# Gate and up of a SwiGLU by Strassen's product, in a one-core transformer layer

## The chip, the core and the metric
The kernel runs on one core of a Trainium2 chip: TensorE (PE, with its weight loads shown as PEld), VectorE (DVE), ScalarE (ACT), GpSimd (POOL) and SyncE (SP), which here issues the DMAs. The metric is the time of one execution on the device in microseconds (us). The core has an on-chip memory of 128 partitions (SBUF) and eight banks of 2 KB a partition (PSUM) into which PE accumulates.

## The reference
One decoder layer on 512 tokens and 16 meta tokens, 1024 channels: sparse attention, a residual and LayerNorm, a SwiGLU of width 2816, a residual and LayerNorm.

```python
def swiglu(h, w_gate, w_up, w_down):
    return (jax.nn.silu(h @ w_gate) * (h @ w_up)) @ w_down
...
h = layer_norm(DEEPNORM_ALPHA * h + mix, ln1_g[i], ln1_b[i])
ffn = swiglu(h, ffn_w_gate[i], ffn_w_up[i], ffn_w_down[i])
h = layer_norm(DEEPNORM_ALPHA * h + ffn, ln2_g[i], ln2_b[i])
```

All is float32. h is (512, 1024), w_gate and w_up are (1024, 2816), w_down is (2816, 1024).

## The kernel before
Each product is made of three matmuls of fp32r parts: a float32 operand x is split into hi, a copy of x on ACT (`act_copy`, L156), and lo = x - hi, a subtraction on DVE or POOL (`sub`, L159); the product is hi*hi + hi*lo + lo*hi (`mm3`, L286 to L288).

The order of the work is the order of the program: `manual_schedule` keeps each engine's instructions as the code issues them, and every engine works its own list from front to back, waiting on semaphores where an operand or a buffer isn't ready. Tiles come from pools by tag with a fixed count of buffers: `q` has 8 (four rows of 528 each), `u` 28, `kq` 14, `lg` 2, the weights `wraw`, `whi` and `wlo` 3 each, and PSUM has the tags `mm` 2, `S` 3, `pt` 2, `av` 1.

After attention come three stages. In the first, the output projection of the second half of the channels goes token block by token block (L968 to L978, blocks b of 128 tokens); `residual` and `norm` work on DVE, POOL and ACT, and `turn_norm` transposes a normalised block on PE and splits it into h1h and h1l. In the second (L991 to L1015), for each of 22 blocks f of 128 columns of w_gate and w_up, PE makes gate into p_wg and up into p_wu, 24 matmuls of 512 tokens each (block 0 in two halves of 256 tokens, so that it can begin before blocks 2 and 3 are normalised). `ahead` loads chunks of weights (128 x 1024) two ahead and cuts one ahead: ACT copies h_wg and h_wu, DVE makes l_wg, POOL l_wu. ACT takes silu of p_wg (L1004), DVE multiplies by p_wu (L1005), and the product is split into hh and hl. At the last block `ahead("wd0_0")` has the first chunk of w_down cut (L1002). In the third (L1037 to L1083), PE multiplies hh and hl with w_down into pd, in two halves th of 256 tokens, and DVE, POOL and ACT do the last normalisation.

Of the kernel before, what the change touches and what calls it, by code (L numbers as in the profile page):

```python
# [117 lines left out]
def trunk(ctx, tc, a, out):  # L118
# [839 lines left out]
    def turn_norm(b):  # L958
        for q in range(2):
            pt = bank(f"tz{b}{q}", "pt")  # L960
            for i in range(4):
# [4 lines left out]
            sub(nc.vector, lo, ptv, hi)

    for b in range(NB):  # L968
        if b:
            po[1, b] = bank(f"po1{b}", "mm")  # L970
        for k in range(0 if b else 6, KT):
            out_terms(1, k, b)
            if b > 1 and k == LATE:
                turn_norm(b - 2)
        residual(1, b)
        norm(b)
        if b == 0:
            load(g_ff, 2)  # L978


    hh, hl = [], []
    hq = []

    def widen(nm, o, n0, n1):
        wh, wl = chunk(nm)
        return mm3(
            o[:, n0:n1],
            ((wh[:, k * P : (k + 1) * P], wl[:, k * P : (k + 1) * P], h1h[k][:, n0:n1], h1l[k][:, n0:n1]) for k in range(KT)),
        )

    for f in range(NF):  # L991
        pg = [bank(f"p_wg{f}", "mm"), bank(f"p_wu{f}", "S")]

        for n0, n1 in ((0, 2 * P), (2 * P, S)) if f == 0 else ((0, S),):
            for o, nm in zip(pg, (f"wg{f}", f"wu{f}")):
                if n1 == S:
                    ahead(nm)
                for k, _ in enumerate(widen(nm, o, n0, n1)):
                    if n1 < S and k == LATER_K:
                        turn_norm(2 + (nm == "wu0"))  # L1000
        if f == NF - 1:
            ahead("wd0_0")  # L1002
        sg = third(f"sg{f}")[:, :S]
        nc.scalar.activation(sg, pg[0], AF.Silu)  # L1004
        nc.vector.tensor_tensor(out=sg, in0=pg[1], in1=sg, op=ALU.mult)  # L1005
        if f < 8:
            if f % 4 == 0:
                hq.append((quad(f"hh{f}", S), quad(f"hl{f}", S)))
            hi, lo = (x[:, f % 4] for x in hq[f // 4])
        else:  # L1010
            hi, lo = unit(f"hh{f}", F32R)[:, :S], unit(f"hl{f}", F32R)[:, :S]
        act_copy(hi, sg)
        sub(nc.vector, lo, sg, hi)
        hh.append(hi)
        hl.append(lo)  # L1015
# [129 lines left out]
```

## Time and profile before

| | us |
|---|---|
| median of 3 executions | 688.37 (687.09 to 688.86) |
| the profiled execution | 688.74 |
| its span | 687.0 |
| PE, DVE, ACT, POOL busy in the span | 668.5, 418.3, 287.6, 244.8 |
| output projection's end to the first down product | 312.4 to 556.4 |
| down products | 556.4 to 672.7 |

Times in rows count from the span's start. The span runs from the first to the last instruction; the execution's own time has some 1.7 us more around it. A busy engine is one that works on an instruction, and a matmul's row is longer than the distance to the next, since matmuls are pipelined: the pace is read from start to start.

### The profile page before, as it was taken

Reading aid. Unit: us, or ns where it says so; the run is one execution under the profiler, and the core shown is the slowest. Engines: PE = TensorE matmul, PEld = TensorE weight load, DVE = VectorE, ACT = ScalarE, POOL = GpSimd, SP = SyncE. Lnnn points to the kernel's source line nnn. Section 1 sums busy time; section 2 is a strip of 40 time slices with the busy share of each in tenths; the row PEclk is TensorE's granted clock in tenths of the full one; section 3 lists DMA queues with packets and bytes.
Section 4 is the critical chain, followed back from the end, with each engine's and each line's share of the span. In section 5 each row is a group of like instructions: output and inputs, shape, how many; then the busy total and the mean of one; then the engine's idle time right before and its main releaser. Section 6 shows DMA issues by size and latency. Waiting matters only on the chain.

```text
span 687.0 us, 9443 instructions
## 1 busy us (share of the span) xinstructions
PE 668.5 (97%) x3440; PEld 564.2 (82%) x3440; DVE 418.3 (61%) x788; ACT 287.6 (42%) x516; POOL 244.8 (36%) x249
## 2 busy tenths in 40 slices
PE   7999999999999999999999999999999999999995
PEld 5888787888998888888888888888888888888884
DVE  5589897898888887686334233343433355575425
ACT  5573512567767675513323233232322344423310
POOL 2063802597786776654212122221212200011004
PEclk9999999999999999999999999999999999999998
DMA  6557131542223245410131322313132267745601
GB/s 235 172 167 253 42 75 37 153 139 79 71 85 109 71 135 189 154 61 29 65 122 62 124 80 104 119 66 123 63 121 90 94 231 234 238 148 198 208 32 61
DMA packets 31806, 83.11 MB, mean 121 GB/s; under 512 B 3744, under 2 KB 8912, under 8 KB 31760
## 3 DMA queue, kind: packets, MB, share of 16 engines
q1 hardware_dynamic: 31328, 82.12, 36.6%
q8 instruction: 27, 0.44, 0.3%
q10 hardware_dynamic: 432, 0.39, 0.2%
q14 instruction: 19, 0.16, 0.1%
HBM read 74.86 MB, written 5.27 MB: 117 GB/s over the span
## 4 chain that ended last, share of the span: by engine, by line
PE 85%; DVE 6%; POOL 3%; ACT 2%; issue 2%; DMA 1%; SPq 0%; POOLq 0%; DVEq 0%; ACTq 0%
PE pd L1063 17%; PE p_wu L287 6%; PE p_wu L286 6%; PE p_wu L288 6%; PE p_wg L287 6%; PE p_wg L286 6%; PE p_wg L288 6%; PE po L771 3%; PE av L726 3%; PE pv L288 2%; PE pv L286 2%; PE pv L287 2%; PE pt L696 2%; PE p_q L288 2%; PE p_q L287 2%
## 5 line engine op out<-in xcount | busy, mean ns | idle before, releaser
L159 POOL TENSOR_TENSOR l_wu<-r_wu,h_wu 128x1024 fp32r<-128x1024 f32 x22 | 52.9, 2405 | 179.5 <-ACT h_wu L156 179.5
L1005 DVE TENSOR_TENSOR sg<-p_wu,sg 128x512 f32<-128x512 f32 x22 | 15.2, 692 | 107.6 <-PE p_wu L288 107.6
L159 DVE TENSOR_TENSOR l_wd<-r_wd,h_wd 128x1024 fp32r<-128x1024 f32 x36 | 45.4, 1263 | 41.2 <-ACT h_wd L156 41.1
L287 PE MATMUL p_wg<-h1l,h_wg 128*128 128x512 f32 (+1 forms) x184 | 70.0, 380 | 0.3 <-DVE h1l L159 0.3
L286 PE MATMUL p_wg<-h1h,h_wg 128*128 128x512 f32 (+1 forms) x184 | 70.0, 381 | 0.0
L286 PE MATMUL p_wu<-h1h,h_wu 128*128 128x512 f32 (+1 forms) x184 | 70.0, 380 | 0.0
L288 PE MATMUL p_wu<-h1h,l_wu 128*128 128x512 f32 (+1 forms) x184 | 69.9, 380 | 0.0
L287 PE MATMUL p_wu<-h1l,h_wu 128*128 128x512 f32 (+1 forms) x184 | 69.9, 380 | 0.0
L288 PE MATMUL p_wg<-h1h,l_wg 128*128 128x512 f32 (+1 forms) x184 | 69.9, 380 | 0.0
L159 DVE TENSOR_TENSOR l_wg<-r_wg,h_wg 128x1024 fp32r<-128x1024 f32 x21 | 52.9, 2518 | 24.4 <-ACT h_wg L156 24.4
L156 ACT ACTIVATE hh<-sg 128x512 fp32r<-128x512 f32 x22 | 13.9, 633 | 119.7 <-DVE sg L1005 119.7
L670 POOL TENSOR_TENSOR lg<-lg,rec 128x144 f32<-128x144 f32 (+1 forms) x64 | 52.6, 846 | 21.9 <-DVE rec L668 21.1
L1063 PE MATMUL pd<-h_wd,hh 128*128 128x512 f32 (+1 forms) x162 | 59.6, 368 | 0.0
L1063 PE MATMUL pd<-h_wd,hl 128*128 128x512 f32 (+1 forms) x162 | 59.6, 368 | 0.0
L1063 PE MATMUL pd<-l_wd,hh 128*128 128x512 f32 (+1 forms) x162 | 59.5, 368 | 0.0
L156 ACT ACTIVATE h_wd<-r_wd 128x1024 fp32r<-128x1024 f32 x36 | 38.1, 1061 | 45.6 <-DMA r_wd<-in_wd 23.2
L644 POOL TENSOR_TENSOR bm<-score,tz 128x256 f32<-128x256 f32 (+1 forms) x64 | 43.9, 717 | 16.4 <-DVE mn L653 14.9
L938 POOL TENSOR_TENSOR fr<-fr,half_neg 128x1 f32<-128x1 f32 x4 | 4.0, 992 | 116.0 <-DVE fr L937 116.0
L661 ACT ACTIVATE lg<-lg,mn 128x272 f32<-128x272 f32 (+1 forms) x64 | 36.3, 571 | 11.6 <-DVE mn L653 11.6
L287 PEld LDWEIGHTS p_wg<-h1l,h_wg 128*128 128x128 f32 x184 | 34.6, 188 | 7.0 <-DVE h1l L159 0.5
L286 PEld LDWEIGHTS p_wg<-h1h,h_wg 128*128 128x128 f32 x184 | 34.6, 188 | 6.9 <-ACT h1h L156 0.2
L288 PEld LDWEIGHTS p_wu<-h1h,l_wu 128*128 128x128 f32 x184 | 34.6, 188 | 6.6
(333 smaller groups left out, 1759.4 us busy)
## 6 DMA issues: line engine op xcount, KB each, us to landing
r_wd<-in_wd SPq DMA_DIRECT2D x36, 512.0 KB, 4.2
r_wg<-in_wg SPq DMA_DIRECT2D x22, 512.0 KB, 3.7
r_wu<-in_wu SPq DMA_DIRECT2D x22, 512.0 KB, 4.5
kb<-ka SPq DMA_DIRECT2D x32, 132.0 KB, 2.3
r_wq<-in_wq SPq DMA_DIRECT2D x8, 512.0 KB, 4.8
r_wk<-in_wk SPq DMA_DIRECT2D x8, 512.0 KB, 3.4
rbig<-rdram SPq DMA_DIRECT2D x1, 3072.0 KB, 15.2
hTr<-in_hT SPq DMA_DIRECT2D x8, 264.0 KB, 5.2
```

The lines of the kernel that those rows point to most:

```text
L156: nc.scalar.activation(o, i, AF.Copy, scale=scale)
L159: eng.tensor_tensor(out=o, in0=x, in1=y.bitcast(F32), op=ALU.subtract)
L286: nc.tensor.matmul(o, lh, rh, start=i == 0, stop=False)
L287: nc.tensor.matmul(o, lh, rl, start=False, stop=False)
L288: nc.tensor.matmul(o, ll, rh, start=False, stop=i == KT - 1)
L644: nc.gpsimd.tensor_tensor(out=bm.at(b, W[b] - n, W[b]), in0=mask.at(b, W[b] - n, W[b]), in1=tzs[h][:, 256 - n :], op=ALU.add)
L661: nc.scalar.activation(lg.blk(b), lg.blk(b), AF.Exp, bias=mn[:, i : i + 1], scale=-1.0, accum_out=den[:, b : b + 1])
L670: nc.gpsimd.tensor_tensor(out=lg.blk(b), in0=lg.blk(b), in1=rec[:, b : b + 1].to_broadcast([P, W[b]]), op=ALU.mult)
L726: nc.tensor.matmul(av[:, 512 - w :], lhs, x[:, c : c + w], start=u == 0 and z == 0, stop=u == 4 and z == len(pr) - 1,)
L771: nc.tensor.matmul(po[hf, b], l[:, bs], r, start=k == 0 and i == 0, stop=k == KT - 1 and i == 2)
L1005: nc.vector.tensor_tensor(out=sg, in0=pg[1], in1=sg, op=ALU.mult)
L1063: nc.tensor.matmul(pd[o], l[:, bs], r[:, c0:c1], start=f == 0 and i == 0, stop=f == NF - 1 and i == 2)
```

## The change
Gate and up are one product of the normalised tokens with [w_gate, w_up], and this product is made block by block in Strassen's form (Winograd's variant). The tokens' matrix is cut into four quarters (256 tokens x 512 channels, `quarter[token half, channel half]`), the weights of a block f into b11 and b21 (gate, first and second 512 channels) and b12 and b22 (up). Seven products of half size take the place of eight: each has 4 x 3 matmuls of 256 columns. Product i of block f multiplies a left part `s{i}` (made once) with a right part `w{f}_{i}` (made for each block).

- Left: s1, s2, s4 are split quarters; s5, s6, s7, s3 are split sums of quarters. S1 is added on DVE, the other three sums are made on POOL (`left_sum`).
- Right, for each block: parts 1, 2, 3 are split weights; parts 5, 6, 7, 4 are split sums T1 to T4, made on POOL (`right_sum`; T4 is written over b21). ACT copies hi, DVE subtracts for lo (`right_part`).
- After the products, DVE adds what stands in PSUM to m, v, u and g (`after`), ACT takes silu of the two halves apart, and POOL multiplies silu and up into `hid`.
- `order` says in which order the products go; blocks 0 and 1 alternate at the start, and from block 2 on it is 6, 5, 2, 7, 4, part 1 of the next block, 3. `prepare` has right parts made LEAD = 5 products ahead and sums EARLY = 4 more.
- `hid` is split in the down stage (`hidden_parts`), 256 tokens at a time, four ahead.
- w_gate and w_up come as wx and wy, loaded by `gate_load`: even blocks into `wraw`, odd blocks into one `q` tile, issued when part 3 of the block two before has been made. Chunks of w_down are no longer in one list with them.
- At the program's start the memset of `diag` stands behind those of `half_neg` and `hm`.

```diff
@@ @@
-LATER_K = 4
+LEAD, EARLY = 5, 4
@@ @@
-        [(f"w{c}{f}", a[f"w{c}"][f], 1024, e) for f in range(NF) for c, e in (("g", "v" if f else "p"), ("u", "p"))]
-        + [(f"wd{th}_{f}", a["wd"][f], 1024, "v") for th in range(2) for f in range(NF - TAIL)],
+        [(f"wd{th}_{f}", a["wd"][f], 1024, "v") for th in range(2) for f in range(NF - TAIL)],
@@ first_outputs, norm of block 0 @@
-                load(g_ff, 0)
-                load(g_ff, 1)
-            if k > 3:
-                cut(g_ff, k - 4)
+                gates.append(gate_load(0))
...
+    def gate_load(f):
+        if f % 2:
+            q = quad(f"gu{f}", 512, F32)
+            x, y = (q[:, 2 * i : 2 * i + 2].rearrange("p j n -> p (j n)") for i in range(2))
+        else:
+            x, y = (raw(f"r_{c}{f}")[:, :1024] for c in ("wx", "wy"))
+        nc.sync.dma_start(x, a["wx"][f])
+        nc.sync.dma_start(y, a["wy"][f])
+        return x, y
@@ turn_norm @@
-            hi, lo = (x[:, :, b * P : (b + 1) * P] for x in h1[q])
-            act_copy(hi, ptv)
-            sub(nc.vector, lo, ptv, hi)
+            for i in range(2):
+                act_copy(
+                    halves_of(quarter[b // 2, q][i])[:, :, b % 2 * P : b % 2 * P + P],
+                    pt[:, i * 256 : i * 256 + 256].rearrange("p (i n) -> p i n", i=2),
+                )
+    def left_part(i, x):
+        q = quad(f"s{i}", 512)
+        hi, lo = (q[:, 2 * j : 2 * j + 2] for j in range(2))
+        for j in range(2):
+            act_copy(hi[:, j], x[j])
+            sub(nc.vector, lo[:, j], x[j], hi[:, j])
...
+    def left_sum(i):
+        if i == 5:
+            sums[1] = [unit(f"S1{j}")[:, :512] for j in range(2)]
+            combine(nc.vector, sums[1], quarter[1, 0], quarter[1, 1], ALU.add)
+            left_part(5, sums[1])
+        elif i == 6:
+            sums[2] = [unit(f"S2{j}")[:, :512] for j in range(2)]
+            combine(nc.gpsimd, sums[2], sums[1], quarter[0, 0], ALU.subtract)
+            left_part(6, sums[2])
...
+    def right_sum(f, i):
...
+        o = b21 if i == 4 else tsum[f][:, 512 * i - 512 : 512 * i]
+        if i in (2, 4):
+            right_sum(f, i // 2)
+        u, v = {1: (b12, b11), 2: (b22, tsum[f][:, :512]), 3: (b22, b12), 4: (b21, tsum[f][:, 512:1024])}[i]
+        nc.gpsimd.tensor_tensor(out=o, in0=u, in1=v, op=ALU.subtract)
+    T_OF = {5: 1, 6: 2, 7: 3, 4: 4}
+    def right_part(f, i):
...
+        act_copy(hi, x)
+        sub(nc.vector, lo, x, hi)
+        if i == 3 and f + 2 < NF:
+            gates.append(gate_load(f + 2))
+    def product(f, i):
...
+        for k in range(4):
+            ks = slice(k * P, (k + 1) * P)
+            for j, (l, r) in enumerate(((wh, sh), (wh, sl), (wl, sh))):
+                nc.tensor.matmul(
+                    o, l[:, ks], r[:, k], start=first and k + j == 0, stop=k == 3 and j == 2,
...
+    def after(f, i):
+        add = lambda o, x, y: nc.vector.tensor_tensor(out=o, in0=x, in1=y, op=ALU.add)
...
+        elif i == 3:
+            add(ev[f, "u"][:, lo], pf[f, "d"], ev[f, "m"][:, hi])
+            hid.append(unit(f"hid{f}")[:, :S])
+            nc.gpsimd.tensor_tensor(out=hid[f], in0=ev[f, "g"][:, :S], in1=ev[f, "u"][:, :S], op=ALU.mult)
+        if i in (4, 7) and {(f, 4), (f, 7)} <= seen:
+            add(ev[f, "g"][:, hi], pf[f, "e"], ev[f, "v"][:, lo])
+            nc.scalar.activation(ev[f, "g"][:, hi], ev[f, "g"][:, hi], AF.Silu)
...
+        if b == 1:
+            prepare(2)
+    left_part(1, quarter[0, 0])
+    left_part(2, quarter[0, 1])
+    prepare(4)
+    for n, (f, i) in enumerate(order):
+        if n == 2:
+            turn_norm(2)
+        if n == 4:
+            turn_norm(3)
+            left_part(4, quarter[1, 1])
+            left_sum(5)
+            left_sum(6)
+            left_sum(7)
+            left_sum(3)
+        prepare(min(n + LEAD, len(order)))
+        product(f, i)
+        if n:
+            after(*order[n - 1])
@@ the loop over 22 blocks (widen, silu, product, split, ahead("wd0_0")) goes @@
@@ down stage @@
+            if o == outs[0]:
+                hidden_parts(th * NF + f + 4)
...
-            for i, (l, r) in enumerate(((hh[f], wh), (hh[f], wl), (hl[f], wh))):
+            xh, xl = parts2[th, f]
+            for i, (l, r) in enumerate(((xh, wh), (xh, wl), (xl, wh))):
```

What this does to the order of instructions is seen at three places. In their rows y31 is the fourth token block's second half, T0 to T4 are tiles of the weight sums of those blocks, q100 to q011 quarters, S10 to S21 left sums, s3 to s7 left parts, w3_7 the right part 7 of block 3.

POOL at the start of the stage, before, from the end of the last normalisation:

```order
L943 TENSOR_TENSOR y31_3292<-y31_3292,b1_1_3332 128x384
L159 TENSOR_TENSOR l_wu1_3882<-r_wu1_3816,h_wu1_3881 128x1024
L159 TENSOR_TENSOR l_wu2_3948<-r_wu2_3885,h_wu2_3947 128x1024
L159 TENSOR_TENSOR l_wu3_4014<-r_wu3_3951,h_wu3_4013 128x1024
L159 TENSOR_TENSOR l_wu4_4081<-r_wu4_4017,h_wu4_4080 128x1024
```

and now, the last of the eight weight sums and the six left sums:

```order
L1042 TENSOR_TENSOR gu1_3573<-gu1_3573,T1_3757 128x512
L1042 TENSOR_TENSOR T0_3753<-r_wy0_3486,r_wx0_3485 128x512
L1042 TENSOR_TENSOR T1_3757<-gu1_3573 128x512
L1008 TENSOR_TENSOR S20_3877<-S10_3868,q000_3641 128x512
L1008 TENSOR_TENSOR S21_3878<-S11_3869,q001_3642 128x512
L1008 TENSOR_TENSOR q100_3800<-q000_3641,q100_3800 128x512
L1008 TENSOR_TENSOR q101_3801<-q001_3642,q101_3801 128x512
L1008 TENSOR_TENSOR q010_3650<-q010_3650,S20_3877 128x512
L1008 TENSOR_TENSOR q011_3651<-q011_3651,S21_3878 128x512
L1042 TENSOR_TENSOR T2_3973<-r_wx2_3969 128x512
```

Where one subtraction of a chunk stood between the last normalisation and the next block, fourteen operations stand now before POOL comes to block 2.

DVE in the middle of the stage, before, one block:

```order
L1005 TENSOR_TENSOR sg3_4073<-p_wu3_4012,sg3_4073 128x512
L159 TENSOR_TENSOR hl0_3876<-sg3_4073,hh0_3875 128x512
L159 TENSOR_TENSOR l_wg5_4111<-r_wg5_4047,h_wg5_4110 128x1024
L1005 TENSOR_TENSOR sg3_4073<-p_wu4_4079,sg3_4073 128x512
L159 TENSOR_TENSOR hl4_4143<-sg3_4073,hh4_4142 128x512
```

and now, from part 2 of block 3 to part 2 of block 4:

```order
L160 TENSOR_TENSOR w3_2_4201<-gu3_4009,w3_2_4201 128x512
L1084 TENSOR_TENSOR sg2_4179<-pe2_4184,v2_4197 128x256
L160 TENSOR_TENSOR w3_7_4220<-T3_4091,w3_7_4220 128x512
L160 TENSOR_TENSOR w3_4_4240<-gu3_4009,w3_4_4240 128x512
L1084 TENSOR_TENSOR uu2_4198<-pd2_4130,m2_4106 128x256
L160 TENSOR_TENSOR w4_1_4259<-r_wx4_4147,w4_1_4259 128x512
L1084 TENSOR_TENSOR m3_4238<-pb3_4243,m3_4238 128x256
L160 TENSOR_TENSOR w3_3_4276<-gu3_4009,w3_3_4276 128x512
L160 TENSOR_TENSOR w4_6_4295<-T4_4223,w4_6_4295 128x512
L160 TENSOR_TENSOR w4_5_4312<-T4_4223,w4_5_4312 128x512
L1084 TENSOR_TENSOR v3_4328<-pb3_4243,m3_4238 128x256
L1084 TENSOR_TENSOR uu3_4329<-pd3_4262,v3_4328 128x256
```

Three operations a block have become twelve, seven of them with both inputs in SBUF. On POOL beside them stand T4 of block 3 (over gu3, behind part 2), T1 and T2 of block 4, hid2, T3 of block 4.

SP at the end of the stage, before:

```order
L188 DMA r_wu21_5171<-in_wu 128x1024
L188 DMA r_wd0_0_5201<-in_wd 128x1024
L188 DMA r_wd0_1_5239<-in_wd 128x1024
L188 DMA r_wd0_2_5269<-in_wd 128x1024
L188 DMA r_wd0_3_5299<-in_wd 128x1024
L844 DMA g2_0_5308<-in_g2 128x512
```

and now:

```order
L845 DMA gu21_6383<-in_wy 128x1024
L855 DMA g2_0_6696<-in_g2 128x512
L855 DMA g2_1_6698<-in_g2 128x512
L855 DMA b2_0_6700<-in_b2 128x512
L855 DMA b2_1_6702<-in_b2 128x512
L188 DMA r_wd0_0_6708<-in_wd 128x1024
```

The first chunk of w_down (r_wd0_0) stood ahead of the loads of the last LayerNorm's rows; it stands behind them now, and the tiles of g2 and b2 take `kq` buffers that m and v of blocks 19 and 20 leave.

## Rows read from the trace of the kernel before

**Rows 1.** The page: busy us, share and instructions by engine; the chain that ended last.
```profile
PE 668.5 (97%) x3440; PEld 564.2 (82%) x3440; DVE 418.3 (61%) x788; ACT 287.6 (42%) x516; POOL 244.8 (36%) x249
...
PE 85%; DVE 6%; POOL 3%; ACT 2%; issue 2%; DMA 1%; SPq 0%; POOLq 0%; DVEq 0%; ACTq 0%
```

**Rows 2.** Table by stretches: us, length, busy us (instructions) by engine, granted clock, DMA.
```profile
9.00:12.00 3.00, 3.00 (x14) 2.62 (x12) 3.00 (x6) 2.77 (x5) 1.12 (x2) 0.50 1.06 406
312.40:319.40 7.00, 6.07 (x48) 5.65 (x47) 5.69 (x12) 2.13 (x4) 4.46 (x6) 1.00 0.00 0
319.40:327.80 8.40, 8.33 (x66) 7.97 (x67) 3.18 (x4) 4.02 (x5) 0.94 (x1) 1.00 0.17 63
328.00:556.40 228.40, 228.40 (x1010) 189.09 (x1009) 84.43 (x65) 66.74 (x85) 50.52 (x21) 1.00 0.28 98
556.40:672.70 116.30, 116.30 (x559) 97.23 (x558) 59.91 (x62) 41.97 (x41) 6.58 (x8) 1.00 0.55 179
```

**Rows 3.** Line L1005 (ns least/median/most, first and last start); timeline of PE, 642.
```profile
L1005 DVE TENSOR_TENSOR sg<-p_wu,sg x22: 691/692/693, 327.9 to 556.4; 128x512 f32<-128x512 f32 x22
...
641.15 0.28 PE L1063 MATMUL pd<-h_wd,hh 128*128 128x256 f32 x1
...
641.85 0.39 PE L1063 MATMUL pd<-h_wd,hh 128*128 128x512 f32 x1
```

**Rows 4.** Timeline of DVE and POOL: start us, us, instruction, idle time before it.
```profile
322.56 1.22 DVE L159 TENSOR_TENSOR l_wg<-r_wg,h_wg 128x1024 fp32r<-128x1024 f32 x1 [0.26 <-ACT h_wg L156]
...
407.36 2.58 DVE L159 TENSOR_TENSOR l_wg<-r_wg,h_wg 128x1024 fp32r<-128x1024 f32 x1 [1.21 <-ACT h_wg L156]
...
406.46 2.41 POOL L159 TENSOR_TENSOR l_wu<-r_wu,h_wu 128x1024 fp32r<-128x1024 f32 x1 [8.49 <-ACT h_wu L156]
```

**Rows 5.** Timeline of DVE and POOL in attention; bd has one input in PSUM.
```profile
274.78 1.58 DVE L159 TENSOR_TENSOR atl<-att,ath 128x512 fp32r<-128x512 f32 x1
276.29 1.63 DVE L159 TENSOR_TENSOR l_wo<-r_wo,h_wo 128x640 fp32r<-128x640 f32 x1
...
275.77 1.47 POOL L159 TENSOR_TENSOR l_wo<-r_wo,h_wo 128x384 fp32r<-128x384 f32 x1
...
255.58 0.80 DVE L159 TENSOR_TENSOR l_wo<-r_wo,h_wo 128x640 fp32r<-128x640 f32 x1
...
256.70 0.68 DVE L711 TENSOR_TENSOR bd<-pt,diag 128x512 fp32r<-128x512 f32 x1
...
255.83 1.44 POOL L670 TENSOR_TENSOR lg<-lg,rec 128x144 f32<-128x144 f32 x2 [0.82 <-DVE rec L668]
```

**Rows 6.** Groups by form: count, busy us, mean ns of one, idle before and releaser.
```profile
L159 POOL TENSOR_TENSOR wol<-r_wr,woh 128x512 fp32r<-128x512 f32 x4 | 5.1, 1294 | 2.7 <-ACT woh L156 2.7
...
L159 DVE TENSOR_TENSOR hl<-sg,hh 128x512 fp32r<-128x512 f32 x22 | 15.2, 692 | 15.4 <-ACT hh L156 15.4
...
L159 DVE TENSOR_TENSOR pt<-pt,pt 128x256 fp32r<-128x256 f32 x16 | 6.7, 417 | 2.0 <-ACT pt L156 1.7
...
L156 ACT ACTIVATE hh<-sg 128x512 fp32r<-128x512 f32 x22 | 13.9, 633 | 119.7 <-DVE sg L1005 119.7
...
L156 ACT ACTIVATE pt<-pt 128x256 fp32r<-128x256 f32 x16 | 6.1, 381 | 0.5 <-PE pt L698 0.2
...
L156 ACT ACTIVATE h_wd<-r_wd 128x1024 fp32r<-128x1024 f32 x36 | 38.1, 1061 | 45.6 <-DMA r_wd<-in_wd 23.2 <-PE pd L1063 18.1 <-issue 1.9
```

**Rows 7.** Timeline of ACT and POOL at the end of the last normalisation.
```profile
317.46 0.71 ACT L941 ACTIVATE y<-y,nm,nr 128x384 f32<-128x384 f32 x1 [4.61 <-POOL nm L939]
324.98 1.28 ACT L1004 ACT_TABLE_LOAD   x1 [2.46 <-PE p_wg L288]
...
319.34 1.00 POOL L943 TENSOR_TENSOR y<-y,b 128x384 f32<-128x384 f32 x1
```

**Rows 8.** DMA issues: count, KB each, median us from issue to landing.
```profile
r_wd<-in_wd SPq DMA_DIRECT2D x36, 512.0 KB, 4.2
...
g<-in_g SPq DMA_DIRECT2D x4, 256.0 KB, 5.2
```

More of the change, by code (lines that the diff above doesn't have):

```diff
@@ L949, in finish_norm, with halves_of @@
             nc.vector.scalar_tensor_tensor(z, z, r, gb[o, q][:, :n], op0=ALU.mult, op1=ALU.add)
-    h1 = [(quad(f"h1h{q}", S), quad(f"h1l{q}", S)) for q in range(2)]
-    h1h, h1l = ([h1[k // 4][i][:, k % 4] for k in range(KT)] for i in range(2))
+    quarter = {}
+    HT = S // 2
+    def halves_of(x):
+        return x.rearrange("p (i n) -> p i n", i=2)
     def norm(b):
@@ L962, in turn_norm @@
                 nc.tensor.transpose(pt[:, i * P : (i + 1) * P], y[b][q][:, i * P : (i + 1) * P], ident)
-            ptv = pt.rearrange("p (i n) -> p i n", i=4)
-            hi, lo = (x[:, :, b * P : (b + 1) * P] for x in h1[q])
-            act_copy(hi, ptv)
-            sub(nc.vector, lo, ptv, hi)
+            if b % 2 == 0:
+                quarter[b // 2, q] = [unit(f"q{b // 2}{q}{i}")[:, :512] for i in range(2)]
+            for i in range(2):
[3 more added lines that the diff above has]
+                )
@@ new lines, in trunk, with combine @@
+    left = {}
+    def left_part(i, x):
[4 more added lines that the diff above has]
+            sub(nc.vector, lo[:, j], x[j], hi[:, j])
+        left[i] = [z.rearrange("p j (i n) -> p (j i) n", i=2) for z in (hi, lo)]
+    def combine(eng, o, x, y, op):
+        for j in range(2):
+            eng.tensor_tensor(out=o[j], in0=x[j], in1=y[j], op=op)
+    sums = {}
+    def left_sum(i):
[7 more added lines that the diff above has]
+            left_part(6, sums[2])
+        elif i == 7:
+            combine(nc.gpsimd, quarter[1, 0], quarter[0, 0], quarter[1, 0], ALU.subtract)
+            left_part(7, quarter[1, 0])
+        else:
+            combine(nc.gpsimd, quarter[0, 1], quarter[0, 1], sums[2], ALU.subtract)
+            left_part(3, quarter[0, 1])
@@ new lines, in trunk @@
+    right, tsum = {}, {}
+    def right_sum(f, i):
+        if (f, i) in tsum:
+            return
+        x, y2 = gates[f]
+        b11, b12, b21, b22 = x[:, :512], x[:, 512:], y2[:, :512], y2[:, 512:]
+        if f not in tsum:
+            tsum[f] = wide(f"T{f}")
+        o = b21 if i == 4 else tsum[f][:, 512 * i - 512 : 512 * i]
[3 more added lines that the diff above has]
+        nc.gpsimd.tensor_tensor(out=o, in0=u, in1=v, op=ALU.subtract)
+        tsum[f, i] = o
@@ new lines, in trunk @@
+    pf = {}
+    def product(f, i):
+        where_to = {1: "a", 2: "a", 6: "b", 7: "b", 5: "d", 3: "d", 4: "e"}[i]
+        first = i in (1, 6, 5, 4)
+        if first:
+            tag = {"a": "mm", "b": "S", "d": ("S", "av")[f % 2], "e": "pt"}[where_to]
+            pf[f, where_to] = bank(f"p{where_to}{f}", tag)[:, :HT]
+        o = pf[f, where_to]
+        (wh, wl), (sh, sl) = right[f, i], left[i]
+        for k in range(4):
[3 more added lines that the diff above has]
+                    o, l[:, ks], r[:, k], start=first and k + j == 0, stop=k == 3 and j == 2,
+                    skip_group_check=not first,
+                )
@@ new lines, in trunk, with prepare @@
+    seen = set()
+    order = [(0, 1), (1, 1), (0, 2), (1, 2)] + [(f, i) for i in (4, 5, 6, 7) for f in range(2)]
+    order += [(0, 3), (2, 1), (1, 3)]
+    for f in range(2, NF):
+        order += [(f, 6), (f, 5), (f, 2), (f, 7), (f, 4)] + [(f + 1, 1)] * (f + 1 < NF) + [(f, 3)]
+    prepared = [0]
+    def prepare(n):
+        for f, i in order[prepared[0] : n]:
+            right_part(f, i)
+        for f, i in order[n : n + EARLY]:
+            if i in T_OF and f < len(gates) and (i != 4 or (f, 2) in right):
+                right_sum(f, T_OF[i])
+        prepared[0] = max(prepared[0], n)
@@ L977, in trunk @@
         if b == 0:
[L978 to L1015, printed above, removed]
@@ new lines, in trunk @@
+            gates.append(gate_load(1))
+        if b == 1:
[17 more added lines that the diff above has]
+            after(*order[n - 1])
@@ L1018, in trunk, with hidden_parts @@
+    after(*order[-1])
     gb2 = {}
     broadcast(("g2", "b2"), gb2)
+    parts2, pq4 = {}, []
+    def hidden_parts(n):
+        while len(parts2) < min(n, 2 * NF):
+            i = len(parts2)
+            if i % 4 == 0:
+                pq4.append(quad(f"hp{i}", 512))
+            x = pq4[-1][:, i % 4]
+            z = hid[i % NF][:, i // NF * HT : i // NF * HT + HT]
+            parts2[i // NF, i % NF] = (x[:, :HT], x[:, HT:])
+            parted(x[:, :HT], x[:, HT:], z, nc.vector)
     last, kept = [], []
@@ L1114 @@
     h = np.concatenate([v["meta_tokens"], v["x"][0]], axis=0)
+    gu = [_by_column(v[f"ffn_w_{c}"][0], NF) for c in ("gate", "up")]
     arrays = {
```

38 lines of the change are left out of this document (31 added, 7 removed).

## The prediction, made before the changed kernel was run
> **What bounds the kernel now.** I read first the page's busy table and the chain of work that ended last: the reader is to see TensorE (PE) busy 97% of the span and holding 85% of the chain [rows 1]. Then the table by stretches, which cuts out what the change touches [rows 2]: from the last output projection of attention (312.4) over the gate and up products (to 556.4) to the end of the down products (672.7). In the long middle stretch, 228.4 us, PE is never idle at the full granted clock, while VectorE (DVE), ScalarE (ACT) and GpSimd (POOL) are busy 84, 67 and 51 us. Then how fast PE goes there: the 22 products of gate and up (L1005) start from 327.9 to 556.4, so 228.5 / 21 = 10.88 us a block, 48 matmuls of 512 columns, 227 ns each. A matmul of 256 columns goes at (641.85 - 641.15) / 6 = 117 ns [rows 3]. So PE binds, and the other engines have slack, on average.
>
> **PE's part of the change.** Each block has 84 matmuls of 256 columns for 48 of 512: 84 x 0.1175 = 9.87 us for 10.88. Over 22 blocks that is 22.2 us less, if PE still sets the pace.
>
> **What the sums cost: the lock.** Per block DVE gets seven subtractions of 512 (both inputs in SBUF) and five additions of 256 (one input in PSUM), POOL five operations of 512 with both inputs in SBUF (four weight sums, one product silu x up). DVE alone takes 0.69, POOL 1.29 [rows 6]. They don't run side by side. The DVE subtraction of 1024 takes 1.22 alone and 2.58 when POOL's, which started 0.9 earlier, is at work: POOL ends at 406.46 + 2.41 = 408.87 and DVE 1.07 behind it [rows 4]. When both have work they alternate: DVE ends at 276.36, POOL's 384 at 277.24 (0.88 later; alone 1.00 [rows 7]), DVE's 640 at 277.92 (0.68 later; 0.80 where it comes first) [rows 5]. So a hand-over hides 0.12 to 0.15, and in alternation a POOL 512 costs 1.16 and a DVE 512 costs 0.55. DVE with one input in PSUM isn't held: 512 in 0.68 over a working POOL [rows 5].
>
> The lock is thus held 5 x 1.16 + 7 x 0.55 = 9.65 us a block, nearly PE's 9.87, before anything is left empty. Now the order that the change gives. Take t = 0 where DVE has subtracted right part 2 of a block. POOL waits for that (T4 is written over b21): T4 1.34. Then, each waiting for the other: part 7 0.55, next block's T1 1.16, part 4 0.55, T2 1.16, part 1 0.55, the hidden product 1.16, part 3 0.55, T3 1.16, part 6 0.55: 8.73. Three of the additions lie beside POOL. POOL's next is T4 again, which waits for part 2: so part 5 0.63, two additions 0.40 and 0.45 (256 from PSUM takes 0.42 [rows 6]) and part 2 0.66 go alone: 10.87 us. Part 7's copy on ACT is queued behind the second silu, which waits for DVE; if T1 therefore takes the lock ahead of part 7, three waits shift and it is about 11.4. I take 11.0. PE has its parts at most five products ahead and must follow. So a round costs as much as a block now (10.88): the 22.2 us are gone, DVE and POOL have become the bound. Bounds of a round: 9.87, if DVE and POOL interleave so that PE binds, and 12.2, if nothing of the hand-over hides (5 x 1.29 + 7 x 0.69 + 0.95).
> The Trainium skill (SBUF — State Buffer, Who interferes with whom) says that a DVE instruction with two SBUF inputs and a GpSimd one that reads SBUF exclude each other, for the whole instruction. The rows show the exclusion, but not the whole instruction [rows 5]; by the rule a round would be the 12.2 just given, by the rows 11.0.
>
> **The start of the stage.** Before, PE had the first half of block 0's matmuls from 312.4 on, since tokens 0 to 255 were split as soon as transposed. Now left_part(1) stands on ACT behind the fourth block's normalisation, which ends at 317.46 + 0.71; PE waits from 312.7 to 318.5. POOL is free at 319.34 + 1.00 = 320.3 [rows 7]. It then has eight weight sums for blocks 0 and 1 and six sums of the left operand. The eight, alternating with seven DVE subtractions: 8 x 1.16 + 7 x 0.55 = 13.1, and some 0.7 where one starts alone: 334.1. The left sums need the transposes of token blocks 2 and 3. Those go through ACT, where the copies stand behind part 4 of block 1, a wait for the sixth weight sum (about 331.1): that part 0.63, a copy and four quarter copies (0.38 each, overlapping; I take 0.3) to 333.3, only now are the two PSUM banks free for block 3's transposes; then two parts, a table load of 1.28 [rows 7], a silu, four quarter copies to 337.6. Left part 4's two copies and subtractions and S1's two additions on DVE: 340.8. Six POOL sums alternate with five subtractions: 6 x 1.16 + 5 x 0.55 = 9.7, 350.5. Behind them on DVE stand the last left parts and only then right part 6 of block 0: 0.55 + 3 x 0.65, so 353. PE has had eight products by then (11.3 us of work in 40) and waits for that one. From 353 to part 2 of block 2 DVE has nine subtractions (5.9), eight additions (3.2) and three POOL operations in between (2.6): 364.6. The first round has one POOL operation more, 11.8: 376.4. Bounds: 5 us less, if sums slip in where DVE waits for ACT, 5 more.
>
> **The rounds and the end.** 18 rounds to part 2 of block 21: 376.4 + 198.0 = 574.4. PE ends its last product 6.3 later. But nothing loads w_down ahead any more: the first load stands on SP's queue behind the four loads of g2 and b2, and b2's last waits for an addition of block 20, 3.3 after part 2. Landing takes 4.2, with the g2 loads of 5.2 in front [rows 8] I take 5.1: 8.5. ACT cuts two chunks (1.06 each [rows 6]) to 10.7, DVE subtracts both to 12.1 (1.22 each) and then the first hidden part, 0.42: 12.5. PE starts the down stage at 574.4 + 12.5 = 586.9, before at 556.4 [rows 2]: 30.5 later. Bounds of this end: 4 less, if the load lands at 4.5, or 2 more. A granted clock of half speed after PE's wait of 6 us, as in 9 to 12 us of the trace [rows 2], would cost 0 to 1.5 (half of the 3 us that it lasted there): I take 0.8.
>
> **Costs taken as nothing.** The down stage splits 44 parts of 256 for none: 0.42 on DVE and 0.38 on ACT a step of 12 matmuls (2.7 us), where DVE has 1.22 and ACT 1.06; POOL is idle there, so no lock; without this cover 9 us. DMA bytes are the same; the loads of odd blocks now wait for part 3 (a rival below). The memsets that swap places at the start lie beside the first DMAs; 0 to 1 us either way.
>
> **Sum.** The profiled execution took 688.74, 0.4 above the median of 688.37. 688.7 + 30.5 + 0.8 = 720.0.
>
> **The rivals.** (1) PE sets the pace of the rounds: DVE's additions all find POOL at work and T4 is never late. For it: 9.65 of lock is under 9.87. Against: POOL must wait for part 2 in each round. 18 x 1.13 less: 700. (2) The other side: PE sets the pace from the first product and the sums hide. For it: DVE 7 x 0.69 + 5 x 0.42 = 6.9 and POOL 6.5 are both below 9.87, and if the lock holds an operation with a ready partner no longer than its own stream they fit. Then 22.2 is gained; paid are the 5.8 before the first product, less the 1.0 that PE stood still in the old start (7.00 + 8.40 with 6.07 + 8.33 busy [rows 2]), and 6.2 before the down stage: 688.7 - 22.2 + 4.8 + 6.2 = 678 (rounded up). It needs rounds under about 10.4 and a start under 5 us. Against: [rows 4, 5]. (3) Nothing of a hand-over hides: 18 x 1.2 more, 742. (4) Weights late: the load of an odd block is issued behind part 3, about 5.2 before T1 needs its first half, and two more loads stand with it; 4.2 is the usual landing. If each of nine comes 1.3 late: 732.
>
> **Chances.** The forecast 0.65 (its own range 709 to 731), rival 1 0.13, rival 2 0.09, rival 3 0.08, rival 4 0.05. Below 687 (faster by over 0.3%, about what can be told from no change): 0.07 of rival 2. Within 0.3%: the 0.02 left of it. Slower: 0.91. The range 697 to 736 holds the forecast and rivals 1 and 4 but for their tails; it leaves out rivals 2 and 3.
>
> **What would show it.** Right: in the middle of the stage DVE subtractions of over 1 us each ended just 0.55 behind a POOL operation, products 6 following at 10.8 to 11.4 us, PE waiting mostly for DVE's parts, over 15 us of PE standing still between 328 and 355, and 5 to 7 us of PE waiting for r_wd, h_wd and the first hp before the first down matmul. Wrong: PE gapless at 9.9 us a block (rival 1), or the first product 6 before 335.

## The result and the profile after

The changed kernel takes 721.25 us (median of 4, 718.8 to 722.85), the kernel before 687.93 (4 runs): 1.048 times as long, 95% interval 1.0447 to 1.0514. The forecast was 720.0. The profiled execution, the fastest, took 718.8 us.

The page after, the same two lines as in [rows 1]: busy us by engine, and the chain that ended last.

```profile
PE 667.4 (93%) x4184; PEld 593.9 (83%) x4184; DVE 572.9 (80%) x1039; ACT 350.7 (49%) x714; POOL 376.6 (53%) x342
...
PE 49%; DVE 26%; issue 9%; ACT 6%; POOL 6%; DMA 2%; SPq 0%; POOLq 0%; ACTq 0%; DVEq 0%
```

PE fell from 85% of the chain to 49%, DVE rose from 6% to 26%. The same table of stretches as in [rows 2], cut at the steps of the forecast: start, last stretch to part 2 of block 2, first round, 18 rounds, end, down products. The columns are the length, the busy us (and instructions) of PE, PEld, DVE, ACT and POOL, the granted clock, the DMA share and GB/s.

```profile
310.60:350.20 39.60, 19.88 (x113) 18.23 (x112) 28.31 (x31) 18.75 (x40) 28.07 (x20) 0.75 0.04 13
350.20:364.70 14.50, 12.65 (x88) 12.17 (x89) 10.91 (x20) 6.75 (x14) 5.74 (x3) 0.86 0.40 147
364.70:376.60 11.90, 9.24 (x76) 8.86 (x75) 11.56 (x13) 3.62 (x7) 9.70 (x6) 1.00 0.01 1
376.60:571.60 195.00, 189.66 (x1515) 183.22 (x1514) 174.35 (x217) 91.08 (x180) 145.28 (x90) 1.00 0.26 95
571.60:584.00 12.40, 9.74 (x82) 9.54 (x80) 6.15 (x11) 5.51 (x11) 4.17 (x3) 1.00 0.54 170
584.00:700.30 116.30, 115.29 (x548) 96.64 (x549) 73.60 (x105) 54.30 (x83) 6.57 (x8) 0.99 0.53 177
```

In the start PE works half of the time, at a mean clock of 0.75. In the rounds PE looks 97% busy, which tells little: its rows overlap. One round has to be read (DVE, then POOL and PE; from block to block it repeats within 0.04 us). In order, DVE's rows are part 7, part 4, uu, part 1 of the next block, m, part 3, parts 6 and 5, and behind the cut part 2, sg and the next part 7. POOL's are T1, T2, the hidden product, T3, T4.

```profile
475.33 0.69 DVE L160 TENSOR_TENSOR w<-T,w 128x512 fp32r<-128x512 f32 x1 [1.00 <-ACT w L157]
476.13 1.60 DVE L160 TENSOR_TENSOR w<-r_wy,w 128x512 fp32r<-128x512 f32 x1
477.65 0.41 DVE L1084 TENSOR_TENSOR uu<-pd,m 128x256 f32<-128x256 f32 x1
477.99 1.45 DVE L160 TENSOR_TENSOR w<-gu,w 128x512 fp32r<-128x512 f32 x1
479.36 0.41 DVE L1084 TENSOR_TENSOR m<-pb,m 128x256 f32<-128x256 f32 x1
479.69 1.43 DVE L160 TENSOR_TENSOR w<-r_wy,w 128x512 fp32r<-128x512 f32 x1
481.05 2.38 DVE L160 TENSOR_TENSOR w<-T,w 128x512 fp32r<-128x512 f32 x2
...
484.14 0.68 DVE L160 TENSOR_TENSOR w<-gu,w 128x512 fp32r<-128x512 f32 x1
484.74 0.42 DVE L1084 TENSOR_TENSOR sg<-pe,v 128x256 f32<-128x256 f32 x1
486.16 0.69 DVE L160 TENSOR_TENSOR w<-T,w 128x512 fp32r<-128x512 f32 x1 [1.00 <-ACT w L157]
...
475.39 1.79 POOL L1042 TENSOR_TENSOR T<-gu 128x512 f32<-128x512 f32 x1
477.26 1.63 POOL L1042 TENSOR_TENSOR T<-gu,T 128x512 f32<-128x512 f32 x1
478.85 1.73 POOL L1101 TENSOR_TENSOR hid<-sg,uu 128x512 f32<-128x512 f32 x1
480.54 1.74 POOL L1042 TENSOR_TENSOR T<-gu 128x512 f32<-128x512 f32 x1
484.97 1.30 POOL L1042 TENSOR_TENSOR gu<-gu,T 128x512 f32<-128x512 f32 x1 [2.69 <-DVE w L160]
...
479.82 1.70 PE L1075 MATMUL pb<-s,w 128*128 128x256 f32 x12 [0.30 <-DVE m L1084]
481.36 1.60 PE L1075 MATMUL pe<-s,w 128*128 128x256 f32 x12
482.80 1.60 PE L1075 MATMUL pa<-s,w 128*128 128x256 f32 x12
```

T1 ends at 475.39 + 1.79 = 477.18, part 4 on DVE at 477.73: 0.55 behind. T2 ends at 478.89, part 1 at 479.44; the hidden product at 480.58, part 3 at 481.12. This is the alternation of [rows 4, 5], four times a round, 1.70 a pair. T4 and part 7 follow each other in the same way: T4 ends at 484.97 + 1.30 = 486.27 and part 7 at 486.85; T1 ends 1.16 behind part 7 (476.02 to 477.18). A product that waits for nothing takes 1.44 (481.36 to 482.80), so seven take 10.08; the round takes 10.83. PE's waits from 376 to 572 (us in all, times, longest):

```profile
PE pb L1075 <- DVE m L1084: 5.3, 18, 0.3
PE pd L1075 <- DVE uu L1084: 1.1, 1, 1.1
```

PE thus waits for no right part. In each round it waits for the addition of m, which stands in DVE's list between the subtractions and has to read the bank of product 6 before product 7 is added there. The end, on SP, ACT, DVE and PE ([rows 8] has the loads before):

```profile
571.86 3.22 SPq L855 DMA_DIRECT2D b<-in_b  x2
575.12 10.66 SPq L188 DMA_DIRECT2D r_wd<-in_wd  x5
...
581.34 1.06 ACT L157 ACTIVATE h_wd<-r_wd 128x1024 fp32r<-128x1024 f32 x1 [0.52 <-DMA r_wd<-in_wd]
...
584.03 0.49 PE L1216 MATMUL pd<-h_wd,hp 128*128 128x512 f32 x1 [2.69 <-ACT hp L157]
...
585.82 0.73 PE L1216 MATMUL pd<-h_wd,hp 128*128 128x512 f32 x2 [0.98 <-DVE hp L160]
```

### The profile page after: what moved, and what is told of

It is laid out like the page before. It is cut to its first block, busy times and chain, and to the rows that moved or that the text cites. A ratio compares the mean times of both kernels' runs of the same rounds, so it can differ in the third digit from the quotient of the medians.

```text
span 717.0 us, 11620 instructions
## 1 busy us (share of the span) xinstructions
PE 667.4 (93%) x4184; PEld 593.9 (83%) x4184; DVE 572.9 (80%) x1039; ACT 350.7 (49%) x714; POOL 376.6 (53%) x342
## 4 chain that ended last, share of the span: by engine, by line
PE 49%; DVE 26%; issue 9%; ACT 6%; POOL 6%; DMA 2%; SPq 0%; POOLq 0%; ACTq 0%; DVEq 0%
PE pd L1216 16%; DVE w L160 16%; ACT w L157 4%; PE po L771 3%; PE av L726 3%; PE pv L288 2%; PE pv L286 2%; PE pv L287 2%; PE pt L696 2%; PE p_q L288 2%; PE p_q L287 2%; PE p_q L286 2%; POOL T L1042 1%; PE p_k L286 1%; PE p_k L288 1%
## 5 line engine op out<-in xcount | busy, mean ns | idle before, releaser
L1216 PE MATMUL pd<-h_wd,hp 128*128 128x512 f32 (+1 forms) x324 | 92.4, 370 | 3.7 <-ACT hp L157 2.7
L1075 PE MATMUL pa<-s,w 128*128 128x256 f32 x528 | 74.9, 295 | 11.8 <-ACT s L157 5.7
L1075 PE MATMUL pb<-s,w 128*128 128x256 f32 x528 | 73.8, 291 | 12.4 <-DVE m L1084 6.9
L160 DVE TENSOR_TENSOR w<-T,w 128x512 fp32r<-128x512 f32 x66 | 66.8, 1039 | 22.6 <-ACT w L157 22.4
L1075 PEld LDWEIGHTS pb<-s,w 128*128 128x128 f32 x528 | 67.4, 195 | 16.7 <-DVE m L1084 10.8
L1075 PEld LDWEIGHTS pa<-s,w 128*128 128x128 f32 x528 | 70.5, 203 | 12.9 <-ACT s L157 6.2
L1075 PE MATMUL pd<-s,w 128*128 128x256 f32 x528 | 72.2, 286 | 3.6 <-DVE uu L1084 2.5
L1075 PEld LDWEIGHTS pd<-s,w 128*128 128x128 f32 x528 | 66.1, 191 | 7.2 <-issue 4.8
L1216 PEld LDWEIGHTS pd<-h_wd,hp 128*128 128x128 f32 x324 | 59.3, 191 | 14.5 <-ACT hp L157 2.9
L1216 PE MATMUL pd<-l_wd,hp 128*128 128x512 f32 (+1 forms) x162 | 60.3, 372 | 0.0
```

The lines of the kernel that those rows point to most:

```text
L160: eng.tensor_tensor(out=o, in0=x, in1=y.bitcast(F32), op=ALU.subtract)
L1075: nc.tensor.matmul(o, l[:, ks], r[:, k], start=first and k + j == 0, stop=k == 3 and j == 2, skip_group_check=not first,)
L1216: nc.tensor.matmul(pd[o], l[:, bs], r[:, c0:c1], start=f == 0 and i == 0, stop=f == NF - 1 and i == 2)
```

## The experiments

Ratios are to the kernel before, run on the same chip beside each version; the changed kernel's is 1.0481. The round is the distance of the additions of m (L1084) in the middle of the stage; 10.83 in the changed kernel.

**All sums on DVE.** In `right_sum`, `left_sum` and for `hid`:

```diff
-        nc.gpsimd.tensor_tensor(out=o, in0=u, in1=v, op=ALU.subtract)
+        nc.vector.tensor_tensor(out=o, in0=u, in1=v, op=ALU.subtract)
```

> All sums of the stage that POOL makes (T1 to T4 of every block, the six left sums, silu x up) are issued on DVE instead; POOL has nothing to do between the last normalisation and the next. Theory of the lock: what costs is that DVE and POOL work in turn, 1.16 + 0.55 us a pair; one engine alone does two operations of 512 in 1.2. A round has 12 x 0.60 + 5 x 0.42 = 9.3 us of DVE, less than PE's own 10.08 (seven products 1.44 apart where it doesn't wait), so PE sets the round at about 10.1 (now 10.83), and the start gets 5 to 8 us shorter: about 701 to 704 us. Theory of the load (no lock in the way, DVE's own queue is what is long; it is at work in 9.8 of 10.8 us): five more operations of 0.6 to 0.69 make the round 11.4 or more, and the time 731 or more.

708.27 us, 1.0284 (1.0255 to 1.0312), 4 above the lock's number. The theory of the load falls: DVE has five more operations a block, and the round is 10.48 where 11.4 was to come. It is 0.4 above the 10.1 of the lock's theory, since in each round DVE still waits 1.0 for a copy that stands on ACT behind the silu:

```profile
455.28 0.42 ACT L1105 ACTIVATE sg<-sg 128x256 f32<-128x256 f32 x1 [2.43 <-DVE sg L1084]
455.61 0.61 ACT L157 ACTIVATE w<-T 128x512 fp32r<-128x512 f32 x1
...
456.25 0.69 DVE L160 TENSOR_TENSOR w<-T,w 128x512 fp32r<-128x512 f32 x1 [1.00 <-ACT w L157]
456.86 0.68 DVE L1042 TENSOR_TENSOR T<-r_wx 128x512 f32<-128x512 f32 x1
```

The rest of a round is 9.48 us of DVE without a gap, operations 0.60 to 0.72 apart.

**T4 alone on DVE.**

```diff
-        nc.gpsimd.tensor_tensor(out=o, ...)
+        (nc.vector if i == 4 else nc.gpsimd).tensor_tensor(out=o, ...)
```

> Only T4 (written over b21) goes from POOL to DVE, where it is issued right behind the subtraction of part 2. Theory of the lock: DVE does T4 in 0.6 in the 1.0 that it now waits, POOL no longer waits 2.7 for part 2 and makes T1 of the next block beside DVE's additions; a round loses one hand-over and comes to 10.1 to 10.4: 708 to 713 us. Theory of the late silu (what binds is the path addition sg on DVE, silu on ACT, copy of part 7 on ACT, subtraction of part 7 on DVE): the addition sg comes 0.6 later, the round is 11.4, and the time 731.

723.66 us, 1.0510 (1.0486 to 1.0534); rounds of 10.75 and 11.25 in turn, 11.0 on average for 10.83. Both numbers missed, the lock's (708 to 713) by 11 and that of the late silu (731) by 7.

**The silu of the second half one product later.** By this edit the silu of block 21's second half comes behind its product silu x up and is missing from the result.

```diff
-            nc.scalar.activation(ev[f, "g"][:, hi], ev[f, "g"][:, hi], AF.Silu)
+            owed_silu.append(ev[f, "g"][:, hi])
...
         prepare(min(n + LEAD, len(order)))
+        late_silu()
         product(f, i)
```

> The silu of the second half is issued on ACT one product later, so that the copy of part 7 doesn't stand behind it. Theory of the late silu: the 1.0 us that DVE waits for that copy in each round is gone, and PE sets the round at 10.1: 707 us. Theory of the lock: part 7's subtraction is then ready while POOL works on T4, and is held until T4 has ended plus 0.55, when it ends now: round 10.7 to 10.9, time 719 to 722.

718.51 us, 1.0434 (1.0412 to 1.0456), round 10.79: DVE's wait of 1.0 is gone, and the round gained 0.04 of it, as the theory of the lock had it. Part 7 now stands from 462.26 to 464.00, held by T4, which ends at 463.45 (0.55 apart).

**No sums of weights from block 2 on.**

```diff
-            right_sum(f, T_OF[i])
-            x = tsum[f, T_OF[i]]
+            if f < 2:
+                right_sum(f, T_OF[i])
+                x = tsum[f, T_OF[i]]
+            else:
+                x = {5: gates[f][0][:, 512:], 6: gates[f][1][:, 512:], 7: gates[f][0][:, 512:], 4: gates[f][1][:, :512]}[i]
```

> From block 2 on the sums T1 to T4 are left out (the parts 5, 6, 7 and 4 are split from the weights as loaded): POOL has one operation a block in the place of five, all else is there, DVE has the same work. Theory of the lock: DVE does its seven subtractions and five additions in about 7 us, PE sets the round at 10.1: 18 x 0.75 = 13.5 less, 707 us. Theory of the load on DVE or of the late silu: the round stays at 10.8, 720 us.

703.31 us, 1.0211 (1.0196 to 1.0226), where 707 was expected; round 10.08, and PE without a wait from 380 to 540:

```profile
455.17 1.60 PE L1078 MATMUL pd<-s,w 128*128 128x256 f32 x12
456.61 1.60 PE L1078 MATMUL pa<-s,w 128*128 128x256 f32 x12
458.05 1.60 PE L1078 MATMUL pb<-s,w 128*128 128x256 f32 x12
```

DVE and ACT have the same work in this run; only POOL's four sums are gone, as partners on the lock and as something to wait for. So 10.08 is PE's own, and 0.75 of each round is what these sums cost. That it is the lock and not the waiting for the sums, the run with all sums on DVE and the late silu shows (below): it has the sums and the same 10.08.

**T4 on DVE and the late silu together** (both diffs above, block 21's silu included).

> T4 on DVE, as in the run that made it slower (round 11.2), and the silu of the second half one product later. Theory: the lock was right on T4 and the path through the silu spoiled it; with the copy of part 7 freed from the silu, the lock is held four times by POOL and eight times by DVE, 4 x 1.16 + 8 x 0.55 = 9.0, with 1 us of additions beside nothing: 10.1 to 10.4, first down product 8 to 13 earlier than now, 709 to 714. Rival (a second path, T1 and T2 of the next block that now meet parts 5 and 6 on the lock, holds it too): round 10.8 to 11.3, 718 or more.

713.77 us, 1.0387 (1.0363 to 1.0411). The time fits the theory, its round doesn't: 10.2 to 10.5 and 10.75 in turn. POOL shows why odd and even blocks differ:

```profile
470.11 1.84 POOL L1042 TENSOR_TENSOR T<-gu 128x512 f32<-128x512 f32 x1 [2.59 <-DMA gu<-in_wx]
472.71 1.54 POOL L1042 TENSOR_TENSOR T<-gu,T 128x512 f32<-128x512 f32 x1 [0.77 <-DMA gu<-in_wy]
```

As soon as T4 holds POOL up no longer, T1 of an odd block waits for its weights (23.2 us in nine blocks); in even blocks T1 and T2 take the lock ahead of parts 6 and 5, and PE's product 3 waits 0.84 for the addition uu behind them. This is rival 4 of the forecast, hidden before by the wait for part 2.

**Sums on DVE and the late silu together.**

> Both edits together: all sums on DVE, and the silu of the second half one product later (here for block 21 too). Theory: with no lock left, DVE has 9.45 us of work a round and waits 1.0 for the copy of part 7, which is the 10.49 measured with the sums on DVE; without that wait DVE is under PE's 10.08 and PE sets the round: 10.1, 18 x 0.4 = 7 less than 708.3: 701. Rival (additions that products 7 and 3 wait for stand behind the sums on DVE): round 10.4 to 10.5, 707 to 709.

697.82 us, 1.0142 (1.0117 to 1.0167). Round 10.08, no wait of PE from 380 to 540. That is 3 better than expected: two waits of 1.0 for copies, which the run with the sums on DVE still has in the start (at 356.68 and 359.50), are gone as well.

**The load of w_down early.** In `right_part`, before product (21, 4), and ahead of the down stage's loop:

```diff
             gates.append(gate_load(f + 2))
+            if f + 2 == NF - 1:
+                load(g_ff, 0)
+        if i == 3 and f == NF - 2:
+            load(g_ff, 1)
+            load(g_ff, 2)
...
+        if (f, i) == (NF - 1, 4):
+            cut(g_ff, 0)
...
+    hidden_parts(4)
     for th in range(2):
```

> The loads of the first three chunks of w_down are issued behind the last loads of weights instead of behind those of g2 and b2; the first chunk is cut before product 4 of block 21, and the first four hidden parts are made ahead of the second cut. Theory of the late load: PE's 2.7 + 1.0 us of waiting before the down products go, the first of them starts within 1 us of the last product of gate and up, and the clock stays: 3.5 to 5 us less, 716.5 to 718. Rival (PE waits for the hidden parts and the last sums in any case, or the cut delays the last sums): 720 to 722.

717.54 us, 1.0431 (1.0405 to 1.0458), 0.5% less than the changed kernel. The first down product starts at 585.84, 0.16 ahead of the last product's end at 586.00. The late load, the hidden parts behind the second cut and the half clock behind these waits, which this run does not have, cost 3.4 us by the ratio (2.8 in the two traces, from the out-projection's end on), near the 2.69 and 0.98 of PE's waits.

**Blocks 0 and 1 plain.** PLAIN gives each plain product its right part, left part and bank; the left sums are issued later, beside these products.

```diff
+    PLAIN = {10: (1, 1, "a"), 11: (2, 2, "a"), 12: (8, 1, "d"), 13: (3, 2, "d"),
...
-    order = [(0, 1), (1, 1), (0, 2), (1, 2)] + [(f, i) for i in (4, 5, 6, 7) for f in range(2)]
-    order += [(0, 3), (2, 1), (1, 3)]
+    order = [(0, 10), (0, 11), (0, 12), (0, 13), (1, 10), (1, 11), (0, 14), (0, 15), (0, 16), (0, 17)]
+    order += [(1, 14), (1, 15), (1, 12), (1, 13), (1, 16), (1, 17), (2, 1)]
```

> Blocks 0 and 1 are made plainly (eight half products each, split quarters q00, q01, q10, q11 times split weights, no sums), the other 20 as now with the sums on POOL. The four sums of the left operand and their parts are made beside them. Theory of the start (PE waits for fourteen sums on POOL and their partners on DVE before it can go on): PE has 16 products of 1.44 = 23 us from 318.5 on, and DVE and POOL need until some 346 to 348 for block 2; product 6 of block 2 starts at 347 to 350 where it started at 368: 19 to 22 less, 699 to 703. Rival (the start is held by something else: weights that land late, ACT's queue): 712 or more.

705.41 us, 1.0259 (1.0233 to 1.0284): 15.3 us less by the ratio (13.3 in the two traces, from the out-projection's end on), where 19 to 22 were expected. Product 6 of block 2 starts at 351.5. PE still waits 5.74 before its first product, has half clock from 314.7 to 324.9, and waits 2.27 for a part of block 1 that stands on DVE behind left parts 5 and 6.

**PE kept at work in the first wait.**

```diff
+    spare = bank("spare", "av")
+    for _ in range(20):
+        nc.tensor.matmul(spare, ath[7][:, 384:512], wo1[7][0], start=True, stop=True)
     left_part(1, quarter[0, 0])
```

> The changed kernel with 20 matmuls of 512 columns into a bank that nobody reads, put into PE's wait ahead of the first product of gate and up; all else as it is. Theory (in the start the sums on DVE and POOL set the time, and PE's clock there costs nothing): the granted clock is full in the first products, part 2 of block 2 and the end come as they are, 719 to 722. Rival (the half clock in the first products costs its own 3 to 5 us): 716 to 718.

721.74 us, 1.0487 (1.0463 to 1.0511): no change. But the half clock was put off more than taken away: the first product starts at 319.25 with the granted clock at 1.00, and from 320.9 to 324.3 it is 0.50. The first two products take 5.80 (319.25 to 325.05) where they took 6.33 (316.34 to 322.67). The stretch from 314 to 331 in the changed kernel, with 0.60:

```profile
314.00:331.00 17.00, 8.55 (x38) 7.96 (x39) 10.59 (x11) 6.68 (x15) 14.47 (x12) 0.60 0.01 1
```

and in this one, with 0.90:

```profile
314.00:331.00 17.00, 9.89 (x50) 8.14 (x48) 12.03 (x15) 5.41 (x12) 14.39 (x12) 0.90 0.00 0
```

The two stretches don't hold the same work, since the out-projection ends at 313.46 here and at 310.61 in the changed kernel. The first addition of m in block 2 comes 59.3 after that end in the changed kernel, 60.1 here. Only the first wait was filled; the clock fell again in the later ones too. So the run took away half a microsecond of slow work, and what the half clock costs in the start it can't tell.

**All together.** Blocks 0 and 1 plain, sums on DVE, late silu, w_down early (the diffs above).

> All together: blocks 0 and 1 plain, all sums on DVE, the silu one product later, w_down early. Theory: first product 318.5, 16 x 1.44 = 23.0, 20 blocks x 10.08 = 201.6, 0.6 to the down stage, 2 us of waits: first down product at 545.7; from there 130.6 to the end of the span as before the change, 1.8 around it: 678 us, 676 to 684, faster than before the change (688). Rival (a wait comes in a round that the single edits did not show, as the additions on DVE): rounds of 10.4, 685 or more.

686.09 us (10 runs), 0.9976 (0.9962 to 0.9989): 0.2% faster than before, but 8 above the forecast. The rounds are 10.08. What was left was the first wait (5.74, then half clock from 313.7 to 323.9) and two waits of 1.5 and 1.1 at block 2.

**Left parts 1 and 2 and six right parts made during the last output projection.** The second block's transposes move ahead (behind two steps of the fourth block's projection), so that ACT's copies come before the third block's norm. The plain products go in another order and the left sums come later; the diff against the changed kernel, in part:

```diff
-        norm(b)
+        if b == 2:
+            turn_norm(1)
+            left_hi(1, quarter[0, 0])
+        norm(b, mid3 if b == 3 else None)
+        if b == 2:
+            left_hi(2, quarter[0, 1])
+            later.append([])
+            prepare(6, 0)
...
+        if n == 17:
             left_sum(3)
```

> The version with blocks 0 and 1 plain, sums on DVE, late silu and early w_down, and now the left parts 1 and 2 and six right parts of blocks 0 and 1 made during the last output projection (left part 1 ahead of the fourth block's residual), and the left sums later. Theory: PE's 5.7 us of waiting at 311.4 becomes about 1, the half clock behind it (2.7 us) and the two waits of 1.5 and 1.1 at block 2 go: 7 to 10 less than 686.1: 676 to 680. Rival (what DVE does for left part 1 it takes from the fourth block's norm, and PE waits for quarters 10 and 11 instead): 684 to 687.

683.23 us (6 runs), 0.9935 (0.9917 to 0.9952), 3 above the forecast. The first wait went; another grew: m's copy stood on ACT behind left part 3, whose sum had been put just there.

```profile
345.77 0.64 PE L1105 MATMUL pd<-s,w 128*128 128x256 f32 x4
349.80 1.88 PE L1105 MATMUL pa<-s,w 128*128 128x256 f32 x12 [3.39 <-ACT m L157]
```

**Two orders put right.** Against the last version:

```diff
+    def mid2():
+        left_lo(1, quarter[0, 0])
...
-        if b == 3:
-            left_lo(1, quarter[0, 0])
...
-        norm(b, mid3 if b == 3 else None)
+        norm(b, {2: mid2, 3: mid3}.get(b))
...
-        if n == 17:
+        if n == 19:
             left_sum(3)
```

> As the last version, with two orders changed: the last left sum and left part 3 are issued two products later, behind the copy of block 2's m, and the subtractions of left part 1 stand ahead of the third block's norm instead of behind it. Theory: PE's waits of 3.4 for that copy, of 0.9 and 0.4 for left part 1, and the half clock behind the first (1.7) go: 683.2 - 5 to 6 = 677 to 679. Rival (part 3 is then late for its product, or the norms are later by what was moved): 682 to 684.

680.57 us (5 runs), 0.9891 (0.9872 to 0.9911), 1.1% faster than before the change and 1.6 above the forecast.

```profile
PE 655.2 (97%) x4208; PEld 589.7 (87%) x4208; DVE 555.0 (82%) x1135; ACT 350.7 (52%) x708; POOL 190.5 (28%) x226
```

That is the page's first row; the stretch from the first product to the first down product:

```profile
314.20:546.70 232.50, 227.91 (x1890) 226.69 (x1889) 211.51 (x380) 122.52 (x238) 6.95 (x6) 1.00 0.28 100
```

Gate and up take 232.5 us here at full clock; before, from 312.4 to 556.4, 244.0.

## Why the prediction was right, step by step

| step | forecast | measured |
|---|---|---|
| PE, first product after the out-projection's end | 5.8 | 5.73 |
| eight weight sums end | 334.1 | 331.66 |
| six left sums end | 350.5 | 348.97 |
| product (0, 6) | 353 | 350.20 |
| part 2 of block 2 ends | 364.6 | 364.6 |
| first round | 11.8 | 11.86 |
| 18 rounds | 18 x 11.0 | 18 x 10.83 |
| part 2 of block 21 to the first down product | 12.5 | 12.4 |
| first down product | 586.9 | 584.03 |
| from it to the span's end, beyond before | 0.8 | 2.4 |

The mechanism stood: DVE and POOL took turns, and the gain of PE went there, into the start and into the end. That the time was met (the median is 1.3 above it, the profiled execution 1.2 below) is partly luck, since errors cancel: in the profiled execution the out-projection ended 2.0 earlier and the 18 rounds took 3.1 less than in the sum, the stretch before part 2 of block 2 took 2.8 and the down stage 1.6 more.

- *PE's own pace* was mis-sized: 84 matmuls take 10.08 (0.120 each), not 9.87; with 10.88 before, PE had 0.8 a block to gain, 17.6 in all, not 22.2. Rival 1 would have been 703 (18 x 0.92 under 720).
- *The lock* was right, and shown: without POOL's sums the round is PE's 10.08, with all on DVE it falls too. That POOL is merely slow doesn't explain it: by rival 2's sums DVE has 6.9 and POOL 6.5 of work a round, and side by side both would have fitted under 10.08. The hand-over hides what the forecast took: the order that it added up gives 10.87, measured were 10.83. The 0.13 on top, for the case that T1 goes ahead of part 7 (11.4), wasn't needed: part 7 ends 0.58 behind T4, and T1 behind part 7. DVE's wait of 1.0 for part 7's copy costs next to nothing, since POOL does T4 in that time, which would hold part 7 up else. One sign was wrong: PE waits in the rounds for the addition of m, not for parts. The Trainium skill (SBUF — State Buffer, Who interferes with whom) has a DVE instruction with two SBUF inputs contend with GpSimd's reads and calls the shared ports an exclusive lock, which whoever issues first gets for the whole instruction (this last it says of DVE's two-port modes). The trace agrees that the two take turns. With a whole instruction each, a round would be the 12.2 of the prediction; with a round of 10.83, and 0.55 for a DVE operation behind POOL's, the trace doesn't agree on the length.
- *The start*: from the out-projection's end (2.0 earlier here) the steps to 350 ran as forecast, within 1. From there to part 2 of block 2 it took 14.4 for 11.6. DVE waited 1.0 twice for copies on ACT behind a silu, which I had counted in the round and not here, and 1.5 for a copy that itself waited for a sum on POOL. PE was busy 17.0 of the 27 us from 328 to 355: it stood still for 10, not for the over 15 of the prediction's signs. Plain first blocks gave 13 to 15 us back, about what the rounds lose (18 x 0.75 = 13.5); these are the two large losses.
- *The end* was right to 0.1, but PE came to it later than forecast: its last product ended 9.7 after part 2 of block 21 (581.34, the products back to back), not 6.3, and so it waited 2.69 for the down stage where 5 to 7 were expected. The down stage then lost 2.4 for 0.8: 1.0 for hidden parts behind the second cut, the rest at half clock (3.4 us from 586.4). Taking this step away alone gave 0.5%.
- *2.0 us before the out-projection's end* lie outside the forecast's steps. In this execution the clock was full where [rows 2] show 0.50:

```profile
10.00:12.00 2.00, 2.00 (x16) 1.82 (x15) 2.00 (x4) 1.89 (x4) 0.00 (x0) 1.00 1.05 412
```

With these 2.0 the forecast's sum would have been 718.0 for the profiled 718.8; the other three executions took 721 to 722.9. How much of the 2.0 is the change is open: in every trace with the swapped memsets PE's first matmul starts at 1.75, before at 2.45, but in ten versions that share the changed kernel's attention the out-projection ends anywhere from 310.9 to 313.65.

What stays open: how much of the loss in the start is half clock. Filling the first wait took too little of it away to tell.

## What to carry to other kernels

Fewer matmuls are worth only what the other engines leave: before trading PE work for sums, add up the elementwise operations with both inputs in SBUF over DVE and POOL together, as one resource, since spreading them over both made the round longer than giving all to DVE. A scheme with shared operands to prepare wants a stage that doesn't need them to run first (two plain blocks here), and the stage behind it must get its first loads issued ahead of anything that waits. When a wait is taken away, look for the next one in the trace, as happened here: late weights once T4 had left POOL, a copy behind a sum once the first wait had gone.
